# Attention heads taken in pairs, with alternating halves of the TensorE array, in a two-layer float32 encoder

## The chip, the core and the metric

The kernel runs on one core of a Trainium2 chip. The metric is device time in microseconds, the median of several runs of the whole program. A core has five engines with an instruction stream each: TensorE (PE in the rows, with its weight loads as PEld), VectorE (DVE), ScalarE (ACT), GpSimd (POOL) and SyncE (SP), which issues the transfers. They wait for each other through semaphores. PE writes into PSUM, a memory of banks, from which ACT and DVE copy results into SBUF.

## What is computed

Two encoder layers on 256 tokens of width 1024, all in float32. Each layer has attention with 16 heads, an output projection with residual, and a gated MLP. Eight heads ("MLA") have queries and keys of 96 columns, made from low-rank latents, and see all tokens. Eight "dilated" heads have 64 columns, and see three windows of stride 1, 4 and 16, with a position bias:

```python
def reference(x, ...):
    for l in range(DEPTH):
        h = rmsnorm(x, attn_norm[l])
        c_q, c_kv, k_r, q_d, k_d, v_d = jnp.split(h @ w_in[l], split_at, axis=-1)
        o_a = mla_mixer(c_q, c_kv, k_r, cos, sin, ...)        # 8 heads, q and k of 96, v of 64
        ...
        o_b = dilated_attention(q_d, k_d, v_d, rel_bias)      # 8 heads, q, k and v of 64
        mixed = jnp.concatenate([o_a.reshape(B, S, -1), o_b.reshape(B, S, -1)], axis=-1)
        x = x + mixed @ w_out[l]
        x = x + conv_ffn(rmsnorm(x, ffn_norm[l]), w_up[l], conv_w[l], conv_b[l], w_down[l])
```

Per head, attention is `softmax(q k^T) v`. The kernel folds the three windows of a dilated head into one bias table `Bn` over all 256 keys, so that both kinds of head are dense 256 by 256 products.

## The kernel before

**Projections.** Weights arrive by DMA in float32 and are split into a high part `wh` (ACT, L174) and a low part `wl` (DVE, L187), activations likewise (`xh`, `xl`; `mh`, `ml`). A projection is three matmuls of 512 columns per block, high by high, low by high and high by low (`group`, L485 to L487; in the output projection `out_mm`, L917, L919 and L920). They add up in the PSUM tiles `acc`, of which there are four banks.

**One head's chain**, in class `Heads`:
- `turn_qk` (L522): four PE transposes bring q and k of a head (a dilated pair at once) to columns-on-partitions, in bank A. `keep_qk` copies them out, k on ACT (L283, the helper `act`), q with its gain on DVE (L275, the helper `ts`).
- `scores` (L544): two matmuls, 128 queries by 256 keys each, into a bank S. They are plain float32, and the trace shows two passes for each. A dilated head has 64 rows of operands, so it uses half of the array's rows; head e of a pair lies on rows 64e to 64e+63. An MLA head uses 96 of the rows, which counts as the full array.
- `softmax`: for an MLA head a maximum on DVE (L554), for a dilated one bias and extremum in one DVE operation per 128 queries (L560); then two exps on ACT. `normalise` divides on DVE.
- `turn_p` (L581): four transposes of the probabilities, in bank A again; ACT copies them out (L283, `t<-A 128x512`).
- `values` (L592): two matmuls (two passes each) give the head's output, 64 columns, so half of the array's columns: even heads write the lower half of bank O, odd heads the upper half. After an odd head `keep_o` copies O as `mh` (ACT) and `ml` (DVE), the operands of the output projection.

Of bank A there is one, of O one, of S two.

**Order.** The loop at L946 goes through 17 steps. In step n it writes the scores and softmax of head n, `turn_qk` of head n+1, `turn_p` of head n-1, and `values` of head n-2. Between these it strews `COUNTS[n]` of the waiting projection steps (the end of the k projection, the v projection, then the output projection), and `extras` (evacuation and scaling of the dilated q, k and v). `W.fill()` issues the next weight splits. This text is not yet the order on the engines: a scheduler of the tile framework orders the instructions for each engine by its own estimates, so that for instance two of a loop step's parts can change places.

Of the kernel before, what the change touches and what calls it, by code (L numbers as in the profile page):

```python
# [10 lines left out]
F32 = mybir.dt.float32  # L11
# [8 lines left out]
P = 128  # L20
D_MODEL = 1024
SEQ = 256
DEPTH = 2
HEADS = 8
HD = 64
# [19 lines left out]
FFN_HOLD = 4  # L45
assert FFN_LAG <= FFN_HOLD
START = 5
COUNTS = [1, 1, 2, 2, 2, 2, 2, 2, 2, 3, 2, 3, 2, 2, 3, 2, 2]
WARM = 8
FIRST = 5  # L50

# [179 lines left out]
def encoder(ctx: ExitStack, tc: tile.TileContext, wpk, x, prm, cst, oh, rb, pos, out):  # L231
# [10 lines left out]
    def nm(s):  # L242
        uid[0] += 1
        return f"{s}_{uid[0]}"
# [2 lines left out]
        return work.tile([P, 512], F32, name=nm("t2"), tag="t2", bufs=7)  # L247

    def mid():
        return work.tile([P, 256], F32, name=nm("t1"), tag="t1", bufs=5)  # L250

    def nat(n=512, tag="nat", bufs=3):
        return work.tile([P, 2, n], F32, name=nm(tag), tag=tag, bufs=bufs)
# [4 lines left out]
    def bank():  # L258
        return psa.tile([P, 512], F32, name=nm("S"), tag="S", bufs=2)
# [4 lines left out]
    def obank():  # L264
        return psa.tile([P, 512], F32, name=nm("O"), tag="O", bufs=1)
# [237 lines left out]
    def run(steps):  # L503
        for s in steps:
            s()

    class Heads:
        def __init__(self, l, mla, q, k, v, pairs, fq=None):
# [2 lines left out]
            self.gain = gqk[:, l, 0:1] if mla else gqk[:, l, 1:2]  # L511
            self.st = [State() for _ in range(HEADS)]

        def turn_qk(self, i):
            if not self.mla and i % 2:
                return
            pt = tbank()
            n = QK if self.mla else 2 * HD
            for o, src in ((0, self.qn), (SEQ, self.kn)):
                for t in range(2):  # L520
                    x = src[:, t, i, :] if self.mla else src[:, t, i * HD:(i + 2) * HD]
                    nc.tensor.transpose(pt[:n, o + t * P:o + t * P + P], x, ident)  # L522
            self.pt = pt

        def keep_qk(self, i):
            if not self.mla and i % 2:
                return
            st, pt = self.st, self.pt
            n = QK if self.mla else 2 * HD
            parts = [mid()[:n], mid()[:n]]  # L530
            act(parts[1], pt[:n, SEQ:], AF.Copy)
            ts(parts[0], pt[:n, :SEQ], self.gain[:n], ALU.mult)
            if self.mla:
                st[i].qk = parts
            else:
                for e in range(2):
                    st[i + e].qk = [z[e * HD:(e + 1) * HD] for z in parts]

        def scores(self, i):
            s = self.st[i]  # L540
            ps = bank()
            for t in range(2):
                o, sl = ps[:, t * SEQ:(t + 1) * SEQ], slice(t * P, t * P + P)
                mm(o, s.qk[0][:, sl], s.qk[1], start=True, stop=True)  # L544
            s.ps = ps

        def softmax(self, i):
            s = self.st[i]
# [35 lines left out]
            act(s.pt, pt, AF.Copy)  # L584

        def values(self, i):
            s = self.st[i]
            if i % 2 == 0:
                self.o = obank()
            a = (i % 2) * HD  # L590
            for k in range(2):
                mm(self.o[a:a + HD, :SEQ], self.v[:, k, i * HD:(i + 1) * HD], s.pt[:, k * SEQ:(k + 1) * SEQ],  # L592
                   start=k == 0, stop=k == 1)

        def keep_o(self, i):
            if i % 2 == 0:
                return
            m = State()
            m.hi = work.tile([P, 1, SEQ], F32R, name=nm("mh"), tag="mh", bufs=6)
            m.lo = work.tile([P, 1, SEQ], F32R, name=nm("ml"), tag="ml", bufs=6)  # L600
            act(m.hi[:, 0, :], self.o[:, :SEQ], AF.Copy)
            tt(m.lo[:, 0, :], self.o[:, :SEQ], m.hi.bitcast(F32)[:, 0, :], ALU.subtract)
            self.pairs[i // 2 + (0 if self.mla else 4)] = m

    def layer(l, sx, late, bias):
# [26 lines left out]
        def d_evac(i, dst, t, a):  # L632
            act(dst[:, t, :], a, AF.Copy)
            sq = wide()
            act(sq, a, AF.Square)
            nc.vector.tensor_reduce(out=ssd[:, i, t, :], in_=sq.rearrange("p (h d) -> p h d", h=HEADS),
                                    axis=AX.X, op=ALU.add)

        def d_factor(i):
            v = small(16)  # L640
            e64 = small(2)
            if i == 0:
                pts(e64, sx.e1, float(HD), ALU.mult)
# [14 lines left out]
        def v_evac(t):  # L658
            act(vd[:, t, :], a_v[t], AF.Copy, scale=sx.r[:, t:t + 1])
# [238 lines left out]
        for b in bias:  # L898
            b()
        run(gq[1:])  # L900
        run(gk[:START - 1])
        hm = Heads(l, True, qm, km, vbox[0], pairs, fq)
        hm.turn_qk(0)
        hm.keep_qk(0)
        run(gk[START - 1:START])

        accs = []
        started = set()
# [13 lines left out]
        def out_steps(k):  # L922
# [8 lines left out]
        vd = nat(tag="natb", bufs=1)  # L931
        extras = {
            0: [lambda: d_evac(0, qd, 0, a_q[0]), lambda: d_evac(0, qd, 1, a_q[1])],
            1: [lambda: d_factor(0)],
            2: [lambda: d_scale(0, qd, 0)],
            3: [lambda: d_scale(0, qd, 1)],
            4: [lambda: d_evac(1, kd, 0, a_k[0]), lambda: d_evac(1, kd, 1, a_k[1]), lambda: d_factor(1)],
            5: [lambda: d_scale(1, kd, 0)],
            6: [lambda: d_scale(1, kd, 1)],
            8: [lambda: v_evac(0), lambda: v_evac(1)],  # L940
        }
        sf = new_xT()
        gf = par("ffn_norm", l)
        hd = Heads(l, False, qd, kd, vd, pairs)
        seq = [(h, i) for h in (hm, hd) for i in range(HEADS)]
        for n in range(2 * HEADS + 1):  # L946
            todo = steps[:COUNTS[n]]
            del steps[:COUNTS[n]]
            old = seq[n - 2] if n > 1 else None
            prev = seq[n - 1] if n else None  # L950
            cur = seq[n] if n < 2 * HEADS else None
            nxt = seq[n + 1] if n + 1 < 2 * HEADS else None
            if cur:
                cur[0].scores(cur[1])
            if prev:
                prev[0].normalise(prev[1])
            if cur:
                cur[0].softmax(cur[1])
            W.fill()
            if nxt:  # L960
                nxt[0].turn_qk(nxt[1])
                nxt[0].keep_qk(nxt[1])
            for e in extras.get(n, []):
                e()
            half = -(-len(todo) // 2)
            run(todo[:half])
# [7 lines left out]
        hd.values(HEADS - 1)  # L974
        hd.keep_o(HEADS - 1)
        run(ou[5][2:3])
        W.fill()

# [212 lines left out]
```

## Time and profile before

| | us |
|---|---|
| median of 3 runs (663.16 to 663.32) | 663.27 |
| the profiled execution: span | 661.9 |
| PE busy | 652.5 |
| DVE busy | 504.3 |
| ACT busy | 398.5 |
| attention, layer 0: 62.28 to 143.53 | 81.25 |
| attention, layer 1: 384.35 to 465.50 | 81.15 |

How to read it: the profile is of one execution, and the span is its time from the first instruction to the last; the median also holds what lies around it. An attention stretch runs from the first score matmul of a layer to the end of its output projection's part that is interleaved with heads. In both stretches the granted TensorE clock is 1.00 and PE is busy for the whole of it, ACT for 50 us and DVE for 54. Busy time of PE contains the changes between ways of using the array, which are no instructions: they show only as a longer distance between two starts. In a timeline row the second column is the time from the first instruction's start to the last one's end in the group; matmuls are pipelined, so a row's duration overlaps the next one's, and what a matmul costs is the distance between starts.

### The profile page before, as it was taken

The page shows a single profiled execution, that of the slowest core. Times are in us where ns is not written, and L with a number is a line of the kernel's source. Part 1 is how long each engine was busy: PE and PEld are TensorE (multiplying, and loading weights), DVE is VectorE, ACT ScalarE, POOL GpSimd, SP SyncE. Part 2 cuts the span into 40 slices and gives each one's busy share as a digit, 9 for nine tenths or more (in the row PEclk, how much of TensorE's full clock was granted, in tenths as well). Part 3 has the DMA queues.
Part 4 walks back from the last instruction along what each step waited for, and adds up shares of the span by engine and source line. Part 5 has one row for each costly group of instructions (what it writes and reads, how often), then busy time and mean ns, then how long its engine had stood idle before and what let it go on. Part 6 is the DMA issues. An engine that isn't in the chain of part 4 may idle for free.

```text
span 661.9 us, 10654 instructions
## 1 busy us (share of the span) xinstructions
PE 652.5 (99%) x4018; PEld 564.1 (85%) x4018; DVE 504.3 (76%) x1050; ACT 398.5 (60%) x721; POOL 40.9 (6%) x109
## 2 busy tenths in 40 slices
PE   8999999999999999999999999999999999999997
PEld 7967776679999999999899877666899999999996
DVE  4798768569977777777699978655898777777773
ACT  5984757656655555555478667645585555555551
POOL 2850000001000000000001100000100000000000
PEclk9999999999999999999999999999999999999999
DMA  8759604215555555554337542311156544555401
GB/s 294 265 199 166 248 0 168 88 64 192 190 192 192 191 184 178 178 178 162 133 124 266 184 182 73 118 65 64 65 193 233 181 174 181 189 188 191 160 1 63
DMA packets 17707, 105.19 MB, mean 159 GB/s; under 512 B 2102, under 2 KB 3799, under 8 KB 6648
## 3 DMA queue, kind: packets, MB, share of 16 engines
q1 hardware_dynamic: 17656, 104.51, 45.6%
q8 instruction: 31, 0.51, 0.3%
q14 instruction: 20, 0.16, 0.1%
HBM read 103.20 MB, written 1.31 MB: 158 GB/s over the span
## 4 chain that ended last, share of the span: by engine, by line
PE 91%; POOL 3%; DVE 2%; DMA 1%; issue 1%; ACT 1%; SPq 1%; DVEq 0%
PE S L1017 12%; PE S L1016 12%; PE S L1018 12%; PE acc L1060 6%; PE acc L1061 6%; PE acc L1062 6%; PE S L544 5%; PE O L592 5%; PE acc L486 5%; PE acc L485 5%; PE acc L487 5%; PE acc L917 3%; PE A L581 2%; PE acc L919 2%; PE acc L920 2%; PE A L522 2%
## 5 line engine op out<-in xcount | busy, mean ns | idle before, releaser
L174 ACT ACTIVATE wh<-raw 128x1024 fp32r<-128x1024 f32 (+3 forms) x188 | 193.2, 1035 | 131.0 <-PE S L1017 65.5
L187 DVE TENSOR_TENSOR wl<-raw,wh 128x1024 fp32r<-128x1024 f32 (+3 forms) x188 | 223.2, 1190 | 42.6 <-ACT wh L174 41.9
L1016 PE MATMUL S<-xh,wh 128*128 128x256 f32 x640 | 180.8, 283 | 0.0
L1017 PE MATMUL S<-xl,wh 128*128 128x256 f32 x640 | 180.8, 283 | 0.0
L1018 PE MATMUL S<-xh,wl 128*128 128x256 f32 x640 | 180.7, 282 | 0.0
L1017 PEld LDWEIGHTS S<-xl,wh 128*128 128x128 f32 x640 | 122.4, 191 | 1.7
L1016 PEld LDWEIGHTS S<-xh,wh 128*128 128x128 f32 x640 | 122.1, 191 | 1.7
L1018 PEld LDWEIGHTS S<-xh,wl 128*128 128x128 f32 x640 | 122.4, 191 | 0.0
L280 DVE SCALAR_TENSOR_TENSOR t<-t,prm_s,t 128x255 f32<-128x255 f32 x176 | 73.8, 477 | 1.0 <-ACT t L283 0.9
L1060 PE MATMUL acc<-wh,mh 128*128 128x512 f32 x176 | 70.0, 397 | 0.0
L1061 PE MATMUL acc<-wh,ml 128*128 128x512 f32 x176 | 69.5, 395 | 0.0
L1062 PE MATMUL acc<-wl,mh 128*128 128x512 f32 x176 | 69.2, 393 | 0.0
L485 PE MATMUL acc<-wh,xh 128*128 128x512 f32 (+2 forms) x160 | 61.2, 382 | 0.9 <-ACT nat L283 0.9
L486 PE MATMUL acc<-wh,xl 128*128 128x512 f32 (+2 forms) x160 | 59.5, 372 | 0.0
L487 PE MATMUL acc<-wl,xh 128*128 128x512 f32 (+2 forms) x160 | 59.0, 369 | 0.0
L283 ACT ACTIVATE t<-t,prm_s 128x256 f32<-128x256 f32 x88 | 47.9, 587 | 6.1 <-DVE t L271 6.1
L283 ACT ACTIVATE t<-A 128x512 f32<-128x512 f32 (+2 forms) x56 | 28.1, 502 | 38.5 <-PE A L522 26.4
L283 ACT ACTIVATE mh<-t 128x256 fp32r<-128x256 f32 x44 | 18.3, 416 | 48.2 <-DVE t L271 48.2
L271 DVE TENSOR_TENSOR t<-S,r2b 128x512 f32<-128x512 f32 (+1 forms) x42 | 28.0, 666 | 25.0 <-PE S L1018 24.8
L1062 PEld LDWEIGHTS acc<-wl,mh 128*128 128x128 f32 x176 | 33.0, 188 | 8.1
L1060 PEld LDWEIGHTS acc<-wh,mh 128*128 128x128 f32 x176 | 33.2, 189 | 6.1
L1061 PEld LDWEIGHTS acc<-wh,ml 128*128 128x128 f32 x176 | 33.1, 188 | 5.9
(168 smaller groups left out, 984.7 us busy)
## 6 DMA issues: line engine op xcount, KB each, us to landing
raw<-in_wpk_dram SPq DMA_DIRECT2D x86, 1024.0 KB, 4.8
raw<-in_wpk_dram SPq DMA_DIRECT2D x3, 896.0 KB, 4.5
raw<-in_wpk_dram SPq DMA_DIRECT2D x3, 768.0 KB, 5.7
raw<-in_wpk_dram SPq DMA_DIRECT2D x2, 816.0 KB, 5.7
Bn<-scr SPq DMA_DIRECT2D x8, 192.0 KB, 11.8
raw<-in_wpk_dram SPq DMA_DIRECT2D x2, 720.0 KB, 6.0
X<-in_x_dram SPq DMA_DIRECT2D x4, 256.0 KB, 5.9
raw<-in_wpk_dram SPq DMA_DIRECT2D x2, 384.0 KB, 6.0
```

What stands on the lines that cost most here:

```text
L174: self.nc.scalar.activation(hi[:, :n], self.raw[t][:, o:o + n], AF.Copy, scale=1.0 if g is None else g)
L187: self.nc.vector.tensor_tensor(out=lo[:, :n], in0=raw, in1=hi, op=ALU.subtract)
L283: nc.scalar.activation(o, a, f, **kw)
L485: mm(o, lhs.hi[:, k, sl], rh, start=k == 0, stop=False)
L486: mm(o, lhs.lo[:, k, sl], rh, start=False, stop=False)
L487: mm(o, lhs.hi[:, k, sl], rl, start=False, stop=k == ktot - 1)
L1016: mm(o, hi[:, kp], sf.hi[:, k, :], start=k == 0, stop=False)
L1017: mm(o, hi[:, kp], sf.lo[:, k, :], start=False, stop=False)
L1018: mm(o, lo[:, kp], sf.hi[:, k, :], start=False, stop=k == 7)
L1060: mm(o, m.hi[:, 0, sl], hi[:, cs], start=j == 0, stop=False)
L1061: mm(o, m.lo[:, 0, sl], hi[:, cs], start=False, stop=False)
L1062: mm(o, m.hi[:, 0, sl], lo[:, cs], start=False, stop=j == NF - 1)
```

## The change

Heads go in pairs, and the loop has 9 steps for 17.
- `scores(i)` takes two banks S and writes both heads' matmuls. For dilated heads they alternate: first 128 queries of head A, of head B, then the second 128 of A and of B, so that two neighbours use opposite row halves. MLA heads stay one behind the other.
- `values(i)` writes both heads into bank O, alternating: keys 0 to 127 of A, of B, keys 128 to 255 of A, of B; neighbours use opposite column halves.
- Values come one pair after the scores (`prev`) where they came two heads after (`old`).
- `turns(i)` lists the turn_qk calls of a pair: two for MLA, one for a dilated pair. The first two MLA heads are turned before the loop, each followed by one projection step.
- In a loop step: scores of the pair and both softmaxes with a `W.fill()` each, extras, then up to four slots (two turn_p of the pair before, the turn_qk of the next) with the projection steps divided among them, normalise, values.
- `COUNTS` and `extras` are rewritten for 9 steps; the pool `t1` has 9 buffers for 5. Banks stay as they are.

```diff
-COUNTS = [1, 1, 2, 2, 2, 2, 2, 2, 2, 3, 2, 3, 2, 2, 3, 2, 2]
+COUNTS = [2, 4, 5, 4, 4, 4, 5, 4, 3]
...
-        return work.tile([P, 256], F32, name=nm("t1"), tag="t1", bufs=5)
+        return work.tile([P, 256], F32, name=nm("t1"), tag="t1", bufs=9)
...
+        def turns(self, i):
+            return (i, i + 1) if self.mla else (i,)
...
         def scores(self, i):
-            s = self.st[i]
-            ps = bank()
-            for t in range(2):
-                o, sl = ps[:, t * SEQ:(t + 1) * SEQ], slice(t * P, t * P + P)
-                mm(o, s.qk[0][:, sl], s.qk[1], start=True, stop=True)
-            s.ps = ps
+            pair = self.st[i:i + 2]
+            for s in pair:
+                s.ps = bank()
+            order = [(s, t) for t in range(2) for s in pair]
+            if self.mla:
+                order = [(s, t) for s in pair for t in range(2)]
+            for s, t in order:
+                mm(s.ps[:, t * SEQ:(t + 1) * SEQ], s.qk[0][:, t * P:t * P + P], s.qk[1], start=True, stop=True)
...
         def values(self, i):
-            s = self.st[i]
-            if i % 2 == 0:
-                self.o = obank()
-            a = (i % 2) * HD
+            self.o = obank()
             for k in range(2):
-                mm(self.o[a:a + HD, :SEQ], self.v[:, k, i * HD:(i + 1) * HD], s.pt[:, k * SEQ:(k + 1) * SEQ],
-                   start=k == 0, stop=k == 1)
+                for e in range(2):
+                    mm(self.o[e * HD:(e + 1) * HD, :SEQ], self.v[:, k, (i + e) * HD:(i + e + 1) * HD],
+                       self.st[i + e].pt[:, k * SEQ:(k + 1) * SEQ], start=k == 0, stop=k == 1)
...
-        run(gk[:START - 1])
+        run(gk[:START - 2])
         hm = Heads(l, True, qm, km, vbox[0], pairs, fq)
-        hm.turn_qk(0)
-        hm.keep_qk(0)
-        run(gk[START - 1:START])
+        for e in hm.turns(0):
+            hm.turn_qk(e)
+            hm.keep_qk(e)
+            run(gk[START - 2 + e:START - 1 + e])
...
+            slots = []
             if prev:
-                prev[0].turn_p(prev[1])
-            run(todo[half:])
-            if old:
-                old[0].values(old[1])
-                old[0].keep_o(old[1])
+                slots += [lambda e=e: prev[0].turn_p(prev[1] + e) for e in range(2)]
+            if nxt:
+                def turn_next(i):
+                    nxt[0].turn_qk(i)
+                    nxt[0].keep_qk(i)
+                slots += [lambda i=i: turn_next(i) for i in nxt[0].turns(nxt[1])]
+            for i, slot in enumerate(slots):
+                run(todo[i * len(todo) // len(slots):(i + 1) * len(todo) // len(slots)])
+                slot()
+            if cur:
+                for e in range(2):
+                    cur[0].normalise(cur[1] + e)
+            if prev:
+                prev[0].values(prev[1])
+                prev[0].keep_o(prev[1])
```

In the changed kernel the lines are L546 (scores), L582 (turn_p), L591 (values), L523 (turn_qk) and L915, L917, L918 (output projection).

The order that comes out on the engines, at three places. First PE in layer 1, where dilated heads begin. Before, from the values of an odd head on to the next scores (`x2` is two instructions in a row):

```order
L592 MATMUL O_4972<-t_845_4967,nat_4288 64x256 x2
L544 MATMUL S_5026<-t_854_5001,t_853_5000 128x256 x2
L917 MATMUL acc_4886<-wh_4803,mh_4939 128x512
L919 MATMUL acc_4886<-wh_4803,ml_4940 128x512
L920 MATMUL acc_4886<-wl_4859,mh_4939 128x512
L581 MATMUL A_5047<-cst_s,t_849_4982 128x128 x4
L917 MATMUL acc_4888<-wh_4803,mh_4939 128x512
L919 MATMUL acc_4888<-wh_4803,ml_4940 128x512
L920 MATMUL acc_4888<-wl_4859,mh_4939 128x512
L592 MATMUL O_5057<-t_856_5015,natb_4483 64x256 x2
L544 MATMUL S_5060<-t_854_5001,t_853_5000 128x256 x2
```

After, from the second turn_p of a pair on to the next pair's scores:

```order
L582 MATMUL A_4984<-cst_s,t_818_4869 128x128 x4
L591 MATMUL O_5014<-t_847_4979,nat_4288 64x256
L918 MATMUL acc_4888<-wl_4879,mh_4937 128x512
L523 MATMUL A_4997<-cst_s,nat_3890 128x128 x2
L523 MATMUL A_4997<-cst_s,nat_3891 128x128 x2
L591 MATMUL O_5014<-t_849_4989,nat_4288 64x256
L591 MATMUL O_5014<-t_847_4979,nat_4288 64x256
L591 MATMUL O_5014<-t_849_4989,nat_4288 64x256
L915 MATMUL acc_4885<-wh_4877,mh_5019 128x512
L546 MATMUL S_5023<-t_852_5003,t_851_5002 128x256
L546 MATMUL S_5024<-t_852_5003,t_851_5002 128x256
L546 MATMUL S_5023<-t_852_5003,t_851_5002 128x256
```

One head's score visit per loop step has become two heads' alternating matmuls, the value matmuls alternate between the heads' `t_847` and `t_849`, and the first out matmul that takes the new `mh_5019` stands right behind them.

ACT at the same place; `t<-A` are the copies out of bank A, `t,s<-t,s` the exps. Before:

```order
L283 ACTIVATE t_865_5052<-A_5047 128x512
L283 ACTIVATE t_861_5033,s_5035<-t_861_5033,s_5034 128x256 x2
L283 ACTIVATE t_874_5080<-A_5074 128x256
L283 ACTIVATE t_869_5067,s_5069<-t_869_5067,s_5068 128x256 x2
L174 ACTIVATE wh_5197<-raw_4722 128x1024
L283 ACTIVATE t_876_5094<-A_5089 128x512
L283 ACTIVATE mh_5101<-O_5057 128x256
```

After:

```order
L283 ACTIVATE t_840_4947,s_4949<-t_840_4947,s_4948 128x256 x2
L283 ACTIVATE t_843_4958,s_4960<-t_843_4958,s_4959 128x256 x2
L283 ACTIVATE t_847_4979<-A_4974 128x512
L174 ACTIVATE wh_5193<-raw_4735 128x1024
L283 ACTIVATE t_849_4989<-A_4984 128x512
L283 ACTIVATE t_852_5003<-A_4997 128x256
L283 ACTIVATE mh_5019<-O_5014 128x256
```

Copies of A stood between the exps of neighbouring heads; now four exps stand in a row, and the copies of the pair before follow them.

PE at the start of attention in layer 0, where `qm` and `km` are the MLA q and k. Before:

```order
L487 MATMUL acc_843<-wl_807,xh_111 128x512
L485 MATMUL acc_844<-wh_787,xh_111 128x512
L486 MATMUL acc_844<-wh_787,xl_112 128x512
L487 MATMUL acc_844<-wl_807,xh_111 128x512
L485 MATMUL acc_844<-wh_787,xh_111 128x512
L486 MATMUL acc_844<-wh_787,xl_112 128x512
L487 MATMUL acc_844<-wl_807,xh_111 128x512
L522 MATMUL A_869<-cst_s,qm_183 96x128 x2
L522 MATMUL A_869<-cst_s,km_184 96x128 x2
```

After:

```order
L487 MATMUL acc_843<-wl_807,xh_111 128x512
L523 MATMUL A_863<-cst_s,qm_183 96x128 x2
L523 MATMUL A_863<-cst_s,km_184 96x128 x2
L485 MATMUL acc_844<-wh_787,xh_111 128x512
L486 MATMUL acc_844<-wh_787,xl_112 128x512
L487 MATMUL acc_844<-wl_807,xh_111 128x512
L485 MATMUL acc_844<-wh_787,xh_111 128x512
L486 MATMUL acc_844<-wh_787,xl_112 128x512
L487 MATMUL acc_844<-wl_807,xh_111 128x512
L523 MATMUL A_878<-cst_s,qm_183 96x128 x2
L523 MATMUL A_878<-cst_s,km_184 96x128 x2
```

The first turning has moved ahead of six projection matmuls, and a second one stands behind them.

## Rows read from the trace of the kernel before

**Rows 1.** The page: the span, and each engine's busy time
```profile
span 661.9 us, 10654 instructions
...
PE 652.5 (99%) x4018; PEld 564.1 (85%) x4018; DVE 504.3 (76%) x1050; ACT 398.5 (60%) x721; POOL 40.9 (6%) x109
```

**Rows 2.** PE's waits, first and last of five (line waited for, releaser: us, times, longest)
```profile
PE S L426 <- DMA X<-in_x_dram: 1.8, 1, 1.8
...
PE S L426 <- ACT ckv L283: 0.5, 1, 0.5
```

**Rows 3.** Timeline of PE, layer 0, full array (start us, us, engine, line, operation)
```profile
70.45 0.39 PE L485 MATMUL acc<-wh,xh 128*128 128x512 f32 x1
70.68 0.39 PE L486 MATMUL acc<-wh,xl 128*128 128x512 f32 x1
70.91 0.60 PE L581 MATMUL A<-cst_s,t 128*128 128x128 f32 x4
71.34 1.03 PE L544 MATMUL S<-t,t 96*128 96x256 f32 x4
72.21 0.41 PE L522 MATMUL A<-cst_s,qm 128*96 128x128 f32 x2
```

**Rows 4.** Timeline of PE, layer 1, dilated heads: values, scores, out matmuls
```profile
438.91 0.40 PE L920 MATMUL acc<-wl,mh 128*128 128x512 f32 x1
439.24 1.08 PE L592 MATMUL O<-t,natb 128*64 128x256 f32 x4
440.25 1.13 PE L544 MATMUL S<-t,t 64*128 64x256 f32 x4
441.31 0.50 PE L917 MATMUL acc<-wh,mh 128*128 128x512 f32 x1
441.64 0.40 PE L919 MATMUL acc<-wh,ml 128*128 128x512 f32 x1
```

**Rows 5.** Timeline of PE where two heads meet; first in the window 111.475 to 111.490
```profile
111.47 0.49 PE L544 MATMUL S<-t,t 64*128 64x256 f32 x2
...
111.47 1.13 PE L544 MATMUL S<-t,t 64*128 64x256 f32 x6
112.53 1.08 PE L592 MATMUL O<-t,natb 128*64 128x256 f32 x4
...
139.33 1.36 PE L592 MATMUL O<-t,natb 128*64 128x256 f32 x8
140.62 0.50 PE L917 MATMUL acc<-wh,mh 128*128 128x512 f32 x1
```

**Rows 6.** Timeline of ACT and DVE, layer 1 (in brackets: idle time before, and its releaser)
```profile
438.09 1.05 ACT L174 ACTIVATE wh<-raw 128x1024 fp32r<-128x1024 f32 x1
439.04 0.58 ACT L283 ACTIVATE t<-A 128x512 f32<-128x512 f32 x1
440.36 0.39 ACT L283 ACTIVATE mh<-O 128x256 fp32r<-128x256 f32 x1 [0.74 <-PE O L592]
441.94 0.51 ACT L283 ACTIVATE t<-t,s 128x256 f32<-128x256 f32 x1 [1.20 <-DVE s L560]
442.94 0.58 ACT L283 ACTIVATE t<-A 128x512 f32<-128x512 f32 x1
...
441.41 0.42 DVE L560 CUSTOM_DVE_ANT_0 t<-S,Bn 128x256 f32<-128x256 f32 x1 [0.22 <-PE S L544]
```

**Rows 7.** Timeline of PE and DVE at the start of attention in layer 0
```profile
59.30 0.38 PE L522 MATMUL A<-cst_s,qm 128*96 128x128 f32 x2
...
58.01 0.42 DVE L271 TENSOR_TENSOR km<-kro,fk 128x256 f32<-128x256 f32 x1
58.35 3.49 DVE L187 TENSOR_TENSOR wl<-raw,wh 128x1024 fp32r<-128x1024 f32 x3
61.76 0.47 DVE L275 TENSOR_SCALAR t<-A,gqk 96x256 f32<-96x256 f32 x1
```

More of the change, by code (lines that the diff above doesn't have):

```diff
@@ L512, in __init__ @@
             self.st = [State() for _ in range(HEADS)]
+        def turns(self, i):
+            return (i, i + 1) if self.mla else (i,)
         def turn_qk(self, i):
-            if not self.mla and i % 2:
-                return
             pt = tbank()
@@ L525, in keep_qk @@
         def keep_qk(self, i):
-            if not self.mla and i % 2:
-                return
             st, pt = self.st, self.pt
@@ L586, in values @@
         def values(self, i):
-            s = self.st[i]
-            if i % 2 == 0:
-                self.o = obank()
-            a = (i % 2) * HD
+            self.o = obank()
             for k in range(2):
-                mm(self.o[a:a + HD, :SEQ], self.v[:, k, i * HD:(i + 1) * HD], s.pt[:, k * SEQ:(k + 1) * SEQ],
-                   start=k == 0, stop=k == 1)
+                for e in range(2):
+                    mm(self.o[e * HD:(e + 1) * HD, :SEQ], self.v[:, k, (i + e) * HD:(i + e + 1) * HD],
+                       self.st[i + e].pt[:, k * SEQ:(k + 1) * SEQ], start=k == 0, stop=k == 1)
         def keep_o(self, i):
-            if i % 2 == 0:
-                return
             m = State()
@@ L933, in layer @@
             0: [lambda: d_evac(0, qd, 0, a_q[0]), lambda: d_evac(0, qd, 1, a_q[1])],
[L934 to L940, printed above, removed]
+            1: [lambda: d_factor(0), lambda: d_scale(0, qd, 0), lambda: d_scale(0, qd, 1)],
+            2: [lambda: d_evac(1, kd, 0, a_k[0]), lambda: d_evac(1, kd, 1, a_k[1]), lambda: d_factor(1),
+                lambda: d_scale(1, kd, 0), lambda: d_scale(1, kd, 1)],
+            3: [lambda: v_evac(0), lambda: v_evac(1)],
         }
@@ L944, in layer @@
         hd = Heads(l, False, qd, kd, vd, pairs)
-        seq = [(h, i) for h in (hm, hd) for i in range(HEADS)]
-        for n in range(2 * HEADS + 1):
+        seq = [(h, i) for h in (hm, hd) for i in range(0, HEADS, 2)]
+        for n in range(HEADS + 1):
             todo = steps[:COUNTS[n]]
             del steps[:COUNTS[n]]
-            old = seq[n - 2] if n > 1 else None
             prev = seq[n - 1] if n else None
-            cur = seq[n] if n < 2 * HEADS else None
-            nxt = seq[n + 1] if n + 1 < 2 * HEADS else None
+            cur = seq[n] if n < HEADS else None
+            nxt = seq[n + 1] if n + 1 < HEADS else None
             if cur:
                 cur[0].scores(cur[1])
[L955 to L962, printed above, removed]
+                for e in range(2):
+                    cur[0].softmax(cur[1] + e)
+                    W.fill()
             for e in extras.get(n, []):
                 e()
-            half = -(-len(todo) // 2)
-            run(todo[:half])
+            slots = []
             if prev:
-                prev[0].turn_p(prev[1])
-            run(todo[half:])
-            if old:
-                old[0].values(old[1])
-                old[0].keep_o(old[1])
+                slots += [lambda e=e: prev[0].turn_p(prev[1] + e) for e in range(2)]
[8 more added lines that the diff above has]
+            if cur:
+                for e in range(2):
+                    cur[0].normalise(cur[1] + e)
+            if prev:
+                prev[0].values(prev[1])
+                prev[0].keep_o(prev[1])
         run(steps)
-        hd.values(HEADS - 1)
-        hd.keep_o(HEADS - 1)
         run(ou[5][2:3])
```

## The prediction, made before the changed kernel had run

> **What bounds the kernel now.** I read the page's busy table first: TensorE (PE) is busy 652.5 of 661.9 us, ScalarE (ACT) 398.5, VectorE (DVE) 504.3 [rows 1]. Next PE's list of waits: five rows, 5.0 us in all, every one outside the two attention stretches that the change rewrites, 62.28 to 143.53 and 384.35 to 465.50 us [rows 2]. The granted clock is 1.00 there, the 2.4 GHz level. So PE has no wait to give back in attention. The change can gain only by taking time out of PE's own stream, and it loses wherever it makes PE wait. The profiled execution spans 661.9 us; the median is 663.27, so 1.4 lies outside the span.
>
> **What PE's work costs.** I price it by the distance from one start to the next. A projection matmul of 512 columns: 0.23 (70.45 to 70.68). Four transposes: 0.43 (70.91 to 71.34), or 0.109 each. An MLA head's four score passes (two matmuls of 256 float32 columns, two passes each) in full-array mode: 0.87 (71.34 to 72.21), or 0.216 a pass [rows 3]. A dilated head uses half of the array's rows for scores, and every head half of the columns for values. There the four passes take 1.01 (values, 439.24 to 440.25) and 1.06 (scores, 440.25 to 441.31): 0.14 and 0.19 go to the change of mode. The matmul before such a change and the one behind it each take 0.33 for 0.23, so 0.10 is added [rows 4].
>
> Do opposite halves run together at all? The trace of before shows it by accident, where two heads met. At 111.47 two passes have started within a window of 15 ns, and six passes end in 1.06 us, what four take alone. At 139.33 eight value passes of two heads take 1.29 us, where two groups in a row would take about 2 x 0.87 + 0.14 = 1.88 [rows 5]. So overlap is real, and pass against pass complete.
>
> *A rule of the skill.* The Trainium skill, page "TensorE: Matmul & The Clock Gate", section "Part 3: Packing small matmuls — row/col tiling", says that matmuls are "strict FIFO, no reordering". The rows at 111.47 disagree: the program has all four passes of one head before the other's first. The rival "strict order" below gives what the rule would make of this change.
>
> **What the change removes from PE.**
> - *Scores.* 16 dilated heads in two layers, four passes each, are 64; four of them were hidden already (two places like the one at 111.47), so 60 on the path. In alternation half is hidden: 32. 28 x 0.216 = 6.05 us. MLA heads are not alternated: nothing.
> - *Values.* 32 heads, 128 passes. In the order after, every one of the 16 pairs has its values split in two: the first head's first matmul alone, then an out matmul or transposes, then the other three (first fence of the change). Two passes alone, then four passes of which two lie under two others, then two alone: six pass times for eight. 16 x 2 x 0.216 = 6.91, less the 1.17 that the two meetings like the one at 139.33 gave before: 5.74.
> - *Changes of mode.* Dilated score visits fall from 17 to 8, value visits rise from 31 to 32 since each group is split, returns to full mode rise from 34 to 40. By the prices above 14.39 us before, 13.64 after: 0.75.
>
> Sum: 12.5 us out of PE's stream. The extras, the COUNTS table and the deeper t1 pool add no instruction to PE. ACT and DVE have the same work, and their idle share covers it, except as follows.
>
> **What it adds: waits.** Pairs make both heads need ACT at one moment, and the bank A for transposes is still a single one. None of these waits exists in before; each is a walk along the order after with durations from [rows 3, 4, 6].
>
> (a) *An out matmul straight behind its own pair's values.* At eight places the L915 row that follows L591 takes the mh that ACT must still copy from O (first fence). ACT starts that copy 1.12 after the first value pass (439.24 to 440.36), and it takes 0.39 [rows 4, 6]; with 0.05 for the hand-over PE goes on at 1.56, where it would have been free at 1.01. 8 x 0.55 = 4.4. Before always had other matmuls there.
>
> (b) *The second turn_p waits for bank A.* ACT copies the first head's turned p only behind the current pair's four exps (second fence). From the first score pass: first exp +1.69 (440.25 to 441.94), 1.00 per head (441.94 to 442.94), so the copy starts at 3.69 and ends at 4.27 with its 0.58 [rows 4, 6]. PE comes to the second turn_p after the scores (1.06), four transposes (0.43) and ten matmuls (2.3): 3.8. It waits 0.5. Six places have ten matmuls between: 3.0. One has eight: 0.95. One has its exps behind three weight splits: 0.6. At the last MLA pair of layer 1 only three matmuls stand between: 1.75. The other pairs I put at 0.06 each, 0.5. Together 6.8.
>
> (c) *A dilated turn_qk waits for the second copy*, which has a wh split of 0.95 ahead of it (438.09 to 439.04 [rows 6]) on ACT, in three places: 3 x 0.3 = 0.9.
>
> (d) *The start in layer 0.* The first turn_qk stands 1.4 us earlier (third fence), at 57.9. Its km is ready at 58.43 (58.01 + 0.42): 0.5. The second goes through the same bank A, which the gain multiply on DVE must empty first, behind two wl splits of 1.16 from 58.35 (3.49 for three): 58.35 + 2.33 + 0.47 = 61.15, where PE is there at about 58.43 + 0.44 + six matmuls (1.4) = 60.3 [rows 7]: 0.85. Behind it 0.25 is saved, since the first scores no longer stand right behind their copy. 1.1.
>
> (e) *Smaller ones*: MLA pairs whose scores need bank S while the pair before is still in its exps, and the tail: 1.4 together, an estimate with 0 and 3 as its ends.
>
> Sum of waits: 4.4 + 6.8 + 0.9 + 1.1 + 1.4 = 14.6. The nearest rows bound it. Below: if ACT reaches each copy as early as it does now, (b), (c) and (e) go and about 6.5 is left. Above: if every exp chain starts later by the 0.3 that one wl split can add to a DVE step, 18.
>
> *A second rule.* The Trainium skill, page "TensorEngine Tiling (Array Packing)", section "PSUM Bottleneck", says that tiling speeds up TensorE but not the emptying of PSUM, whose copies may become the bottleneck. The copies of [rows 6] keep their 0.58 and 0.39 whatever PE does, which is what (a) and (b) price; without the rule the sum is the same.
>
> **Forecast.** 661.9 - 12.5 + 14.6 + 1.4 = 665.4; I say 665.3. PE's stream gets shorter by 12.5 and gets back as much in waits: a dilated pair's period falls from 9.3 us to about 8.3 where its PE work alone is 7.3, but with fewer matmuls in it than before, so that the total is level or a little longer.
>
> **Rivals.**
> 1. *ACT is there in time; faster.* If the exps, and with them the copy, stand as early as PE needs (DVE's softmax steps begin as soon as the first head's passes end, not both heads'), bank A is free when the second turn_p comes. The chain would have to be shorter by 0.5 of 4.3 us. For: ACT is busy only 60% [rows 1]. Against: in the program the copy stands behind all four exps, and the exps cannot start before the scores. Then (a), (d) and 1.0 are left, 6.5: 661.9 - 12.5 + 6.5 + 1.4 = 657.3.
> 2. *Strict order; slower.* If the alternating passes do start in program order, pairs of halves still overlap, but each matmul's second pass holds up the other half's first: a score group's last pass then starts one and a half passes later (0.32 x 8 = 2.6), a value group's by 0.05 (16 x 0.05 = 0.8). 665.3 + 3.4 = 668.7. Against it stands [rows 5].
> 3. *It does not do what it says; slower.* If alternating matmuls share the array less than those two meetings did, for instance because both halves' weight loads queue, the 11.8 us of passes stay: 677. It decides if a dilated pair's eight score passes take over 1.5 us.
>
> **How the numbers follow.** The forecast's mechanism has 70%, rival 1 13%, rival 2 12%, rival 3 5%. Inside the forecast the waits of 14.6 are the unsure term: plus or minus 3.5 gives 661.5 to 668.8. The range goes on to 660 and 669.5, which leaves out most of rival 1 and all of rival 3. About 0.2%, 1.3 us, is what a measurement can tell here: faster means under 661.9. Faster: rival 1 and a seventh of the forecast, 0.23; same (to 664.6): a third of the forecast, 0.25; slower: the rest, 0.52.
>
> **What would show it.** Right: attention stretches of 81 to 83 us in spite of an S visit of two heads in about 1.1 us; new rows in PE's waits, bank A and L582 released by ACT (about 0.5 each, some ten times), and L915 released by ACT's mh (about 0.55, eight times); ACT's copy of A at 3.7 us behind a pair's first score pass. Wrong: no A row in the waits (rival 1), score pairs of 1.4 us (rival 2) or 1.9 (rival 3). A different clock, or stretches outside attention that move by over 1 us, would be nothing I have priced.

## The result, and the profile of the changed kernel

The changed kernel takes 668.02 us (median of 4 runs, 667.33 to 670.55) where the kernel before takes 663.24: a ratio of 1.0079, interval 1.0061 to 1.0097. It is slower, as forecast, and inside the range (660.0 to 669.5), but by 4.8 us where 2.0 were forecast. The profiled execution spans 665.6 us, against 661.9 in [rows 1].

The page's head, and TensorE's waits (line waited for, releaser: us in all, times, longest):

```profile
span 665.6 us, 10649 instructions
...
PE 643.6 (97%) x4018; PEld 555.2 (83%) x4018; DVE 507.8 (76%) x1050; ACT 398.2 (60%) x721; POOL 38.6 (6%) x109
```

```profile
PE A L582 <- ACT t L283: 4.0, 9, 1.6
PE acc L915 <- ACT mh L283: 3.8, 8, 0.5
PE O L426 <- DVE X L271: 2.5, 2, 1.2
...
PE A L523 <- DVE t L275: 1.0, 1, 1.0
...
PE A L523 <- ACT t L283: 0.6, 3, 0.2
```

PE is busy 8.9 us less than before, and none of these five rows has an answer in [rows 2]. The first, second and fifth are the bank A and mh waits of the forecast, at nine, eight and three places; the fourth is the start of layer 0. The third was not forecast: in each layer, behind attention, the last transposes of x wait 1.2 us for a residual sum.

One dilated pair of layer 1, on PE and then on ACT (start us, us, engine, line, operation; in brackets idle time and its releaser):

```profile
436.60 0.50 PE L915 MATMUL acc<-wh,mh 128*128 128x512 f32 x1 [0.47 <-ACT mh L283]
437.03 1.13 PE L546 MATMUL S<-t,t 64*128 64x256 f32 x8
438.09 0.66 PE L582 MATMUL A<-cst_s,t 128*128 128x128 f32 x4
...
440.69 0.40 PE L917 MATMUL acc<-wh,ml 128*128 128x512 f32 x1
441.33 0.65 PE L582 MATMUL A<-cst_s,t 128*128 128x128 f32 x4 [0.24 <-ACT t L283]
...
444.92 0.50 PE L915 MATMUL acc<-wh,mh 128*128 128x512 f32 x1 [0.47 <-ACT mh L283]
```

```profile
438.72 0.51 ACT L283 ACTIVATE t<-t,s 128x256 f32<-128x256 f32 x1 [2.18 <-DVE s L561]
...
440.21 0.50 ACT L283 ACTIVATE t<-t,s 128x256 f32<-128x256 f32 x1
440.61 0.19 ACT L283 ACTIVATION_READ_ACCUMULATOR t<-t,s 128x1 f32 x1
440.71 0.57 ACT L283 ACTIVATE t<-A 128x512 f32<-128x512 f32 x1
441.18 1.04 ACT L174 ACTIVATE wh<-raw 128x1024 fp32r<-128x1024 f32 x1
```

Read from the scores at 437.03: both heads' eight passes take 1.06 us (to 438.09), as long as one head's four in [rows 4]. The first exp is at +1.69 and the copy of A at +3.68; the walk had 1.69 and 3.69. PE comes to the second L582 and starts it at +4.30 (4.32 in the walk). From 436.60 to 444.92 the pair takes 8.32 us, where 8.3 was forecast. The waits list counts idle time from the modelled end of the matmul before: 0.24 at 441.33, where the distance between starts, 0.64 for 0.23, shows 0.41.

Where the time went, by starts on PE (a table of mine from the two timelines, us):

| | before, layer 0 / 1 | after, layer 0 / 1 |
|---|---|---|
| first score to last values matmul | 78.03 / 77.92 | 78.10 / 80.44 |
| last values to first MLP matmul | 6.56 / 6.56 | 7.41 / 7.41 |
| from there to the next layer's first score | 237.48 | 236.86 |
| from the second layer's to the end | 193.03 | 192.83 |

With the start (the first score stands at 62.28 before, at 62.52 after) this adds up to the 3.7 us between the spans. The rows do not hold the same matmuls in both kernels. By a count of the two timelines the change moves, in each layer, four projection matmuls (0.23 us each) behind the first score and four transposes (0.11) ahead of it, three out matmuls (0.23) ahead of the last values, and three transposes of x ahead of the first MLP matmul. So the third row, 0.6 us shorter, also holds less work, and the second row, 0.85 us longer, holds 0.70 us less of out matmuls and 0.33 more of transposes: like for like it costs about 1.2 us a layer.

### The profile page after: what moved, and what is told of

It reads as the page before. It is cut to its first block, busy times and chain, and to the rows that moved or that the text cites. A ratio compares the mean times of both kernels' runs of the same rounds, so it can differ in the third digit from the quotient of the medians.

```text
span 665.6 us, 10649 instructions
## 1 busy us (share of the span) xinstructions
PE 643.6 (97%) x4018; PEld 555.2 (83%) x4018; DVE 507.8 (76%) x1050; ACT 398.2 (60%) x721; POOL 38.6 (6%) x109
## 4 chain that ended last, share of the span: by engine, by line
PE 83%; ACT 5%; DVE 5%; POOL 3%; issue 2%; DMA 1%; SPq 1%; DVEq 0%; ACTq 0%
PE S L1013 12%; PE S L1012 12%; PE S L1014 11%; PE acc L1056 6%; PE acc L1057 6%; PE acc L1058 6%; PE acc L486 4%; PE acc L485 4%; PE acc L487 4%; ACT t L283 4%; PE O L591 3%; PE S L546 3%; PE A L523 2%; POOL s L291 2%; PE acc L915 1%
```

## The experiments

Times are medians, beside the kernel before on the same chip (663.35 to 663.45 in the three groups of runs).

| kernel | us | ratio to before (interval) | span |
|---|---|---|---|
| after_again | 667.61 | 1.0061 (1.0049 to 1.0073) | 666.3 |
| s_headwise | 673.10 | 1.0152 (1.0137 to 1.0168) | 670.7 |
| copy_dve | 663.61 | 1.0005 (0.9996 to 1.0013) | 661.6 |
| steps_behind | 676.60 | 1.0198 (1.0172 to 1.0223) | 674.8 |
| behind_dil | 673.26 | 1.0145 (1.0129 to 1.0160) | 673.2 |
| behind_dil_dve | 668.87 | 1.0078 (1.0054 to 1.0102) | 669.0 |
| after_tail | 668.92 | 1.0088 (1.0072 to 1.0103) | 669.0 |
| v_pairs | 656.18 | 0.9893 (0.9878 to 0.9907) | 652.5 |
| v_pairs_hw | 658.07 | 0.9916 (0.9903 to 0.9930) | 656.2 |
| vs_pairs | 650.01 | 0.9802 (0.9788 to 0.9815) | 647.9 |
| vs_pairs_w7 | 648.38 | 0.9784 (0.9762 to 0.9806) | 647.3 |
| vs_w7_tail | 647.52 | 0.9747 (0.9728 to 0.9766) | 645.8 |

**The change once more.**

> The changed kernel once more, unaltered. Its four times lie between 667.33 and 670.55 us, those of the kernel before between 663.16 and 663.32. Theory: the attention stretches are a fixed sequence and repeat to 0.2 us (81.3 and 83.6 us from the first score to the last output-projection matmul), and what varies is the start, before 62 us, where the profile shows a stretch at the lower TensorE clock. Rival: the waits in attention themselves vary, by 1 us or more in a layer.

Both attention stretches repeat to 0.01 us (78.11 and 80.44 from the first score to the last values, then 7.41 twice), and so do those behind them. Only the first score stands elsewhere, at 63.24 for 62.52. That is the whole difference between the spans of 666.3 and 665.6. So the spread between these two profiles is in the start; the run of 670.55 us has no profile (its mean granted clock is 0.995, that of the other three 0.997), and what it lost is open.

**Is it the alternation that overlaps?**

> The changed kernel with the score matmuls of a dilated pair in the order A, A, B, B for A, B, A, B. Theory (a half of the array that is free starts its next matmul whatever stands ahead of it for the other half, as at 111.47 in the kernel before): a pair's scores still take 1.06 us from the first start to the next engine work, and the time stays within 0.7 us of the changed kernel's 667.6. Rival (matmuls start in program order): the second head starts behind the first head's last pass but one, a pair takes 1.4 to 1.9 us, 8 x 0.3 to 0.86, 670 to 674.5.

```diff
-            order = [(s, t) for t in range(2) for s in pair]
-            if self.mla:
-                order = [(s, t) for s in pair for t in range(2)]
+            order = [(s, t) for s in pair for t in range(2)]
```

A pair's scores in the order A, A, B, B, as a timeline, and the same start in the window 449.168 to 449.185:

```profile
449.17 1.14 PE L544 MATMUL S<-t,t 64*128 64x256 f32 x8
450.24 0.44 PE L580 MATMUL A<-cst_s,t 128*128 128x128 f32 x2
```

```profile
449.17 0.49 PE L544 MATMUL S<-t,t 64*128 64x256 f32 x2
```

Eight passes in 1.07 us, and two are under way within 17 ns (their starts are 13 ns apart, as where two heads meet in [rows 5]; 6 or 7 in the changed kernel). The theory holds: neighbours suffice, and the rival is out. But the time is 5.5 us above after_again, not within 0.7. The scheduler, given the other order, also put other work elsewhere (this pair holds fifteen out matmuls, the same pair in the changed kernel twelve); the waits of the second turn_p rose:

```profile
PE A L580 <- ACT t L283: 7.5, 9, 1.6
```

The number that tells of the halves is the visit's, not the kernel's.

**Does ScalarE's queue hold bank A?**

> The changed kernel, with the first head's turned probabilities copied out of bank A by VectorE and no longer by ScalarE. Theory (bank A is held because the copy stands behind four exps on ScalarE): the copy of dilated pairs ends about 3.2 us behind the first score, ahead of TensorE's 3.9, so the waits of L582 for ACT (nine, 4.0 us) fall to 1 us or less; about 664.5 to 665.5. Rival (another user of the bank, or VectorE as late as ScalarE): L582 waits as long for VectorE, 667 to 669.

```diff
             s.pt = wide()
-            act(s.pt, pt, AF.Copy)
+            if i % 2:
+                act(s.pt, pt, AF.Copy)
+            else:
+                ts(s.pt, pt, 1.0, ALU.mult)
```

DVE and PE in a dilated pair:

```profile
437.00 0.69 DVE L275 TENSOR_SCALAR t<-A 128x512 f32<-128x512 f32 x1
```

```profile
434.45 1.13 PE L546 MATMUL S<-t,t 64*128 64x256 f32 x8 [0.55 <-DVE t L275]
435.52 0.66 PE L582 MATMUL A<-cst_s,t 128*128 128x128 f32 x4
437.74 0.66 PE L582 MATMUL A<-cst_s,t 128*128 128x128 f32 x4
```

The copy now begins 2.55 us behind the first score, for 3.68, and the second L582 has no bracket. L582's nine waits for ACT are gone; one of 0.8 for DVE is left. A pair with the same twelve out matmuls takes 7.54 us (442.27 to 449.81) for 8.32. The kernel is 4.0 us faster than after_again and ends level with the kernel before, at 663.61 even a little below the expected 664.5 to 665.5. The theory holds.

**Is the mh wait a cost of its own?**

> The changed kernel, with one constraint: a pair's projection steps may not be issued ahead of the pair's scores on TensorE. An output matmul then no longer follows its own pair's values; the next scores do. Theory (wait for the mh copy is an own cost): the eight waits of L915 for ACT's mh, 3.8 us, go, and some 0.15 us for each of about six changes to full-array mode that fall away; 668.0 - 3.8 - 0.9 = about 663.3. Rival (the mh wait only covers ACT's chain): the wait moves on to the transposes of the pair's second head, which now stand as far behind the scores as before, so 666.5 or more.

```diff
-                run(todo[i * len(todo) // len(slots):(i + 1) * len(todo) // len(slots)])
+                part = todo[i * len(todo) // len(slots):(i + 1) * len(todo) // len(slots)]
+                if cur:
+                    with tc.issue_after(cur[0].last.ins):
+                        run(part)
+                else:
+                    run(part)
                 slot()
```

The mh waits vanish from the list, and the kernel is 9 us slower:

```profile
PE A L523 <- DVE t L275: 7.0, 4, 3.0
PE A L583 <- ACT t L283: 6.0, 8, 2.6
PE S L546 <- DVE t L275: 4.3, 6, 0.7
PE acc L1018 <- ACT xh L283: 4.1, 2, 2.0
```

Layer 0 took 83.97 us from first score to last values for 78.11, layer 1 77.60 for 80.44. I put the loss down to the MLA pairs' turns (L523), which stood without cover. That was too simple: L523 waits as long in layer 1 (2.9 us, up to 402.95) as in layer 0 (3.0, up to 71.00), but in layer 0 the granted clock then fell (0.65 from 72 to 80 us) and in layer 1 it did not (1.00 from 400 to 412). Also, seven out matmuls of each layer (1.6 us) had moved behind the last values; summed up to the next layer's first score, or the end, layer 0 lost 9.6 us against after_again and layer 1 gained 0.75. The six runs go from 672.25 us at a mean clock of 0.995 to 679.33 at 0.985, so a part of the 9 us is the clock. The constraint was then confined to dilated pairs (`if cur and n >= 4`):

> As steps_behind, but the constraint holds for the dilated pairs' steps alone. In steps_behind the MLA pairs lost 5.9 us in layer 0, while layer 1 from first score to last values took 77.6 us for 80.4. Theory (the mh wait is an own cost that an order can save; the loss of steps_behind was the MLA pairs' turning left without cover): layer 1 gains 2.5 us or more, layer 0 about 1.5, total 663.5 to 665. Rival (steps that cannot go ahead leave gaps here too): 667 or more.

This missed too: 77.89 and 82.37 us, 673.26 in all. A dilated pair on PE, and DVE ahead of its scores:

```profile
438.38 0.66 PE L583 MATMUL A<-cst_s,t 128*128 128x128 f32 x4 [0.21 <-ACT t L283]
...
440.01 0.66 PE L523 MATMUL A<-cst_s,nat 128*128 128x128 f32 x4
440.59 1.08 PE L592 MATMUL O<-t,nat 128*64 128x256 f32 x6
442.38 1.13 PE L546 MATMUL S<-t,t 64*128 64x256 f32 x8 [0.71 <-DVE t L275]
```

```profile
440.70 1.23 DVE L187 TENSOR_TENSOR wl<-raw,wh 128x1024 fp32r<-128x1024 f32 x1 [2.01 <-ACT wh L174]
441.85 0.48 DVE L275 TENSOR_SCALAR t<-A,gqk 128x256 f32<-128x256 f32 x1
```

The mh wait is gone, and the scores now wait 0.71 us for the turned q, which DVE empties from bank A behind a weight split. A pair takes 8.31 us (442.38 to 450.69), as before the constraint. So in dilated pairs the mh wait lay over another one and cost nothing by itself: the rival's sort of answer, with q in place of the transposes it named. Nor is it the amount of work that sets a pair's time: it is 8.25 us with nine out matmuls (from 112.38 in the changed kernel), 8.32 with twelve and 8.31 with fifteen (from 452.29 in steps_behind), while other pairs with fifteen take 9.19 (from 103.19 in the changed kernel) and 9.86 (from 449.17 in s_headwise), all at a granted clock of 1.00. What counts is where they stand. (This kernel's loss lies elsewhere: ahead of the dilated pairs of layer 1 stand waits of 1.6 and 1.9 us, and the granted clock was 0.50 from 424 to 432 us; the mean clock of its runs is 0.987 to 0.995, of after_again's 0.996 to 0.997.) That pointed to a ring, a chain of steps that ends where it starts, through bank A:

> behind_dil (673.3 us) with the first head's turned probabilities copied by VectorE. In behind_dil the mh waits are gone, yet a dilated pair takes 8.31 us as in the changed kernel (8.32): TensorE waits 0.71 us for the turned q and 0.2 for bank A. Theory (a ring sets the pair's time: scores, four exps, copy, second turn, copy, turn of q and k, next scores, all through the one bank A): the shorter copy shortens the ring, a dilated pair takes 7.4 to 7.7 us. Rival (VectorE's own queue with its weight split sets it): 8.2 or more.

The pairs now start at 429.91, 437.94, 445.74 and 453.34: 8.03, 7.80 and 7.60 us, and the kernel is 4.4 us faster than behind_dil (4.1 between two runs of the same mean clock, 0.987: 670.83 for 674.97). Moving the copy alone shortens the pair, as the ring says, but it reached the stated 7.4 to 7.7 in the last pair only. L546 still waits for DVE's t, 7.4 us in seven places of the kernel, so DVE's queue has a part in the ring.

**The tail behind attention.**

> The changed kernel; the two weight splits that are written into the end of attention may not be issued ahead of the last residual sum on VectorE and the ScalarE work before it. In the changed kernel a wl split of 1.23 us stands ahead of the first residual sum there, and TensorE then waits 1.2 us for X in each layer. Theory (this split's place is the tail's loss): from the last values matmul to the first MLP matmul 6.5 us in each layer for 7.41, as in the kernel before; 1.8 us off, about 665.9. Rival (the weights are then late for the MLP): the wait moves to the first MLP matmuls, 667 to 669.

```diff
         run(ou[5][2:3])
-        W.fill()
...
         W.done(u_out[7])
-        W.fill()
+        with tc.issue_after(late_x[0]), tc.issue_after(late_x[1]):
+            W.fill(2)
```

From the last values to the first MLP matmul it is 7.17 us for 7.41, but the stretches behind grow by 1.0 and 2.3 us over the changed kernel's: the MLP now waits for its weights (ACT's wh, 0.5 us in all, at two places), and in layer 1 the granted clock was 0.72 from 476 to 480 us. The wait of L426 for X stays at 1.1 us: the early split of 1.23 us is not what holds X, or not alone. What the timelines show besides is another order. PE behind attention of layer 0, before, and PE and DVE in the changed kernel:

```profile
144.32 0.48 PE L917 MATMUL acc<-wh,mh 128*128 128x512 f32 x1
...
146.87 0.50 PE L1016 MATMUL acc<-xh,wh 128*128 128x256 f32 x2
...
147.45 0.60 PE L426 MATMUL O<-cst_s,X 128*128 128x128 f32 x4
```

```profile
147.75 0.52 PE L426 MATMUL O<-cst_s,X 128*128 128x128 f32 x3 [1.23 <-DVE X L271]
148.03 0.48 PE L1012 MATMUL acc<-xh,wh 128*128 128x256 f32 x2
...
146.93 0.68 DVE L271 TENSOR_TENSOR X<-acc,X 128x512 f32<-128x512 f32 x1
```

Before, six out matmuls from 144.32 on stand among the transposes of x, and the last four transposes come behind the first MLP matmuls. In the changed kernel the out matmuls are done by then, and three of the last transposes stand ahead of the MLP, where they wait for DVE's last residual sum. In after_tail three out matmuls stand among the transposes again and two of the last transposes ahead of the MLP. That this order is the cause was not tested, so what holds X stays open.

**The overlap without the burst of exps.** The first edit leaves the loop over single heads and holds an even head's values back to the odd head's:

> The kernel before, with its loop over single heads, scores and softmax as they are; only the values of an even head are held back and issued with those of the odd head, alternating column halves. Theory (the overlap is worth its passes, and the change's losses come from the two heads' exps at one moment, not from the values): two heads' values take 1.3 us for 2.0, 0.7 x 14 pairs less 0.4 at each of five pairs that the order splits, 8 us; about 655. Rival (a new wait for the mh copy eats it, as in the changed kernel): 0.5 x 14, about 661 to 662.

```diff
-            s = self.st[i]
-            if i % 2 == 0:
-                self.o = obank()
-            a = (i % 2) * HD
-            for k in range(2):
-                mm(self.o[a:a + HD, :SEQ], ...)
+            if i % 2 == 0:
+                return
+            self.o = obank()
+            for k in range(2):
+                for e in range(2):
+                    h = i - 1 + e
+                    mm(self.o[e * HD:(e + 1) * HD, :SEQ], self.v[:, k, h * HD:(h + 1) * HD], ...)
```

7.2 us faster than before, as the theory had it to 1 us. Layer 0 takes 70.39 us from first score to last values, layer 1 71.14 (with five and three out matmuls fewer than before, which follow later), with no wait above 0.2 us in them. Written A, A, B, B it keeps the overlap:

> v_pairs (656.2 us) with the four value matmuls of a pair in the order A, A, B, B. In s_headwise a dilated pair's scores in that order took 1.07 us, as much as alternating ones. Theory (two groups need only be neighbours): the four take 1.0 to 1.3 us here too; time within 1.5 us of v_pairs, the order of other work aside. Rival (columns are not rows: the second group waits for the first): 1.9 us at each pair, 14 x 0.7, about 665.

```profile
432.35 1.09 PE L593 MATMUL O<-t,natb 128*64 128x256 f32 x8
433.38 0.48 PE L544 MATMUL S<-t,t 64*128 64x256 f32 x1
```

Eight passes in 1.03 us: columns behave as rows do. (By medians the kernel is 1.9 us slower than v_pairs. Between the profiled executions it is 3.7, since that of v_pairs is its fastest run; where most of it lies is shown under "not expected" below.) The second edit pairs the dilated scores at the even head, and leaves each softmax at its step:

> The kernel before, with its loop over single heads; values of a pair together at the odd head (as in v_pairs, 656.2 us), and now also the scores of a dilated pair together, alternating, at the even head, each head's softmax at its own step. Theory (the passes are worth what they were priced at, and the losses come from the exps of two heads at one moment): eight pairs, two visits of 1.06 us become one, 8 x 1.06 less the 1.0 that two of them had already, 7.5 us off; about 648.5, with no new wait for bank A or mh above 0.3 us. Rival (the second head's bank S, now held one step longer, makes the next pair wait, 0.5 us or more each): 653 or more.

```diff
-            s = self.st[i]
-            ps = bank()
-            ...
+            if not self.mla and i % 2:
+                return
+            pair = self.st[i:i + 1] if self.mla else self.st[i:i + 2]
+            for s in pair:
+                s.ps = bank()
+            for t in range(2):
+                for s in pair:
+                    mm(s.ps[:, t * SEQ:(t + 1) * SEQ], s.qk[0][:, t * P:t * P + P], s.qk[1], ...)
```

PE, and the rows of attention in its waits:

```profile
428.00 1.08 PE L595 MATMUL O<-t,natb 128*64 128x256 f32 x8
429.01 1.14 PE L547 MATMUL S<-t,t 64*128 64x256 f32 x8
430.08 0.50 PE L920 MATMUL acc<-wh,mh 128*128 128x512 f32 x1
```

```profile
PE acc L1019 <- ACT xh L283: 4.1, 2, 2.0
...
PE A L522 <- ACT t L283: 0.2, 1, 0.2
PE A L583 <- ACT t L283: 0.2, 1, 0.2
```

650.01 us, 2% faster than before (648.5 was expected), with the overlap of both kinds and 0.4 us of waits for bank A. ACT's order shows why: a copy of A stands between the two heads' exps, not behind them:

```profile
431.21 0.49 ACT L283 ACTIVATE t<-t,s 128x256 f32<-128x256 f32 x1
431.61 0.19 ACT L283 ACTIVATION_READ_ACCUMULATOR t<-t,s 128x1 f32 x1
431.70 0.58 ACT L283 ACTIVATE t<-A 128x512 f32<-128x512 f32 x1
432.36 0.51 ACT L283 ACTIVATE t<-t,s 128x256 f32<-128x256 f32 x1
```

What is left is the wait for xh where the MLP begins, 2.0 us a layer:

> As vs_pairs, with seven buffers of weight halves for six. In v_pairs TensorE waits twice 2.1 us behind attention for xh, since the splits of the next weights stand between the residual sums and the normalised x on VectorE and ScalarE. Theory (buffers set the place of these splits): with one more they run earlier, half of that wait goes, 2 us off vs_pairs. Rival (the order of the tail sets it, not the buffers): within 0.5 us of vs_pairs.

(`W_BUFS = 7` for 6.) The wait stayed at 4.2 us, so the order of the tail sets it, as the rival says, though the medians are 1.6 us apart and not within 0.5; their difference lies within the two runs' spreads (649.66 to 651.10, 647.47 to 652.18).

> vs_pairs_w7 (648.4 us) with the last weight split of attention held behind the residual sums. TensorE's wait for xh at the start of the MLP, 2.1 us in each layer, has wh splits of 1.05 us ahead of xh on ScalarE. Theory: these splits are that wait; 2 to 4 us off, 644.5 to 646.5. Rival (weights late for the MLP): 648 or more.

(The last `W.fill()` of attention under `issue_after`, as in after_tail.) The wait for xh is gone from the list, which leaves 0.8 us for xl. From the last values to the first MLP matmul it is 7.26 us for 8.52 in layer 0 and 7.26 for 8.86 in layer 1; each next stretch gives back 0.5, and the median, 647.52, is 0.9 below vs_pairs_w7: the splits were that wait, but the expected 2 to 4 us did not come. It is the fastest version that ran, 2.5% under the kernel before.

## Why the prediction came out as it did

- **What leaves PE's stream: right.** Visits for dilated scores took 16.28 us before and take 8.52 (8 x 1.06); those for values 31.0 and, without the waits in them, 25.4 (16 x (0.58 + 1.01)). That is 13.3, less 0.6 for six more returns to the full array: 12.7 where 12.5 was forecast. (By the prices as printed the changes of mode come to 14.4 and 14.0 us, a gain of 0.4 for the stated 0.75, and the forecast to 12.2.) All 16 value groups are split 1 + 3, as the order had shown. Rivals 2 and 3 are refuted by one row (437.03, 1.06 us), although the time, 668.0, lies nearer to rival 2's 668.7 than to the forecast: alone it would have named the wrong mechanism. The rule of the Trainium skill (page "TensorE: Matmul & The Clock Gate", section "Part 3: Packing small matmuls — row/col tiling") that matmuls keep strict order does not hold in s_headwise either, with 13 ns between a first pass and one that the program has four passes later.
- **(a) mh: size right, meaning wrong.** Eight waits; the distance between starts is 0.85 for 0.31, so 0.54 each and 4.3 in all (4.4). But the prediction added it as a cost of its own. behind_dil showed that, for dilated pairs, taking it away brings out a wait for q, with the pair at 8.31 us as at 8.32.
- **(b) bank A: the largest wait, a little over-sized.** By distances 6.0 us (6.8); the dilated ones are 0.41 each (0.5), the one at the end of layer 1's MLA heads 1.81 (1.75). copy_dve shows the cause. The Trainium skill's page "TensorEngine Tiling (Array Packing)", section "PSUM Bottleneck", says that copies out of PSUM may become the bound of a tiled TensorE; the runs agree, by the order of the copies more than by their length (0.58 us before, 0.57 after).
- **(c), (d): right in sum.** 0.27 at three places (0.3). At the start 0.22 and 1.13 of waiting (0.5 and 0.85 in the forecast), less the 0.25 saved: 1.1 (1.1). The first score stands 0.24 later than before in the profiled run and 0.96 in after_again, with 0.5 us less work ahead of it.
- **(e) smaller ones and the tail: the step that failed.** They were put at 1.4 together, with 0 and 3 as ends. The sum leaves them 4.2: the 3.7 between the spans, plus 12.7, less the 12.2 of (a) to (d). The stretch behind the last values, which I had not walked, costs 1.2 a layer like for like, 2.4 us, as much as L426 waits for X there. The rest, about 1.8 us, I cannot name one by one: it is spread over gaps such as 0.24 ahead of two MLA scores (72.28 and 81.85) and 0.10 wherever a lone output matmul stands between values and scores (0.43 from 436.60 to 437.03, where two changes of mode meet and 0.33 was priced). Attention as measured in the table ahead of the prediction took 82.2 and 84.5 us, where 81 to 83 were expected.

So the sum missed by a term taken as small because it was not walked, and the forecast of "a little slower" held, since the gain (12.7 for 12.5) and the four walked waits (12.2 for 13.2) were sized to a tenth. That the walked waits came out 1.0 us too large hid a part of what (e) lacked; this part of the agreement is luck.

## What to carry to other kernels

Overlap in array halves came here from standing next to each other, not from alternating, so look for the fewest instructions that must move: here values could wait for their neighbour and scores come early for it, with the softmaxes left where they were, and a change that had lost 0.8% gained 2%. Before pairing whole chains, ask what the pair now needs at one moment: two heads' exps in front of the copy that frees the only transpose bank had a large part in turning 12.7 us of shorter work into waits (6.0 us of (b), and the ring that lengthens the pair). And a wait that is seen last may lie over another: cut the ring (copy_dve), not the wait on top (steps_behind).

## What was not expected of the hardware

- A second group of matmuls on the free half of the array starts 6 to 14 ns behind the first, whatever the program order within the pair, for rows (s_headwise) and columns (v_pairs_hw). Seen here for float32 matmuls of two passes.
- An idle stretch of 2 us can cost more than itself. v_pairs and v_pairs_hw have the same wait of 2.05 us for xh at the MLP's start. Windows of 4 us there (busy us of PE, PEld, DVE, ACT, POOL, granted clock, DMA share, GB/s), v_pairs first:

```profile
136.00:140.00 4.00, 2.91 (x17) 2.13 (x15) 3.89 (x6) 3.47 (x6) 0.00 (x0) 1.00 0.13 16
140.00:144.00 4.00, 3.04 (x26) 3.04 (x27) 3.76 (x7) 2.65 (x8) 0.00 (x0) 1.00 0.64 252
```

```profile
136.00:140.00 4.00, 2.65 (x16) 1.93 (x14) 3.89 (x7) 3.73 (x7) 0.00 (x0) 1.00 0.08 12
140.00:144.00 4.00, 3.29 (x17) 3.30 (x18) 3.25 (x5) 2.14 (x7) 0.00 (x0) 0.65 0.65 250
144.00:148.00 4.00, 4.00 (x33) 4.00 (x33) 0.86 (x2) 0.41 (x2) 0.81 (x3) 0.93 0.02 4
```

In the second the granted clock fell for some us to the lower of its two levels (1.2 GHz for 2.4) after the wait, in the first it did not. The stretch to the next layer's first score took 239.78 us for 238.20, and the one at the end 195.25 for 193.71: 1.5 us each time. steps_behind shows the same after its waits (clock 0.65 from 72 to 80 us). It is not a matter of the kernel alone. In vs_pairs, one execution, TensorE has this wait in both layers (2.0 us each), and the clock fell behind the first (0.72 from 140 to 144 us) and not behind the second (1.00 from 456 to 460). And of the four runs of v_pairs the profiled one, 654.32 us, has a mean clock of 1.000, the others, 656.14 to 656.62 us, of 0.994 to 0.997. What decides, no run here settles.
